# Scaling x in place ahead of plain transposes, with later weight splits and two store queues, in a two-layer decoder trunk

## The chip, the cores and the metric

The kernel runs on one core of a Trainium2 chip. The metric is the device time of one execution in microseconds (us). TensorE multiplies matrices and transposes, VectorE and ScalarE do elementwise work, GpSimd fills constants, and SyncE (SP) issues the DMAs. Each engine takes its instructions in the order in which the code issues them.

## What is computed

A trunk of two residual layers on x of 256 tokens by 2048 channels, batch 1. Layer 0 is an RWKV-7 token mixer, layer 1 a differential attention; each has a gate path and an output projection. Only the start of layer 0 and the very end matter here:

```python
def rms_norm(x, w, eps):
    y = xf * lax.rsqrt(jnp.mean(xf * xf, axis=-1, keepdims=True) + eps)
    return y * w
...
h = rms_norm(x, norm_w[i], NORM_EPS)
h_prev = jnp.pad(h, ((0, 0), (1, 0), (0, 0)))[:, :T]
xs = h[None] + (h_prev - h)[None] * mu[:, None, None, :]      # six mixed inputs
proj = jnp.einsum('pbtd,dpe->pbte', jnp.stack([x_r, x_k, x_v, x_g]), w_in.reshape(D, 4, RWKV_WIDTH))
...
x = x + y                                                     # after each layer
return rms_norm(x, final_norm_w, NORM_EPS)
```

## The kernel before

**The large products.** A weight tile holds 2 x 128 rows by 512 columns of a weight matrix. `fetch` loads it from DRAM on SP's queue, `high` (ScalarE, L196) casts it to a short type, `low` (VectorE) makes the remainder, and a product step multiplies high and low parts: 24 matmuls of 128 x 256 in layer 0's first products. `gemm` runs eight such steps for one block of 512 output columns. `RAW` = 4 raw tiles and `LEAD` + 1 = 4 split tiles are held. In step `i0`, `gemm` first fetches tile `i0 + 5`, then issues the matmuls, then `high(i0 + LEAD)`, then a piece of each live stream (`pump`), then `low(i0 + LEAD)`.

**The operand of the first products.** x lies in `xin` with tokens on the partitions, in two blocks of 128 tokens, t = 0 and 1. ScalarE squares it as its loads land, and the root of the mean gives `rs0`, one factor for each token. For each pair kp of 128-channel blocks (eight pairs), a generator `first_pairs` does three pieces of work, here called flip, mix and finish:

- `flip(kp)`: TensorE brings the pair to channels on the partitions, into a PSUM bank; ScalarE copies it to `ht` (L310). Before the change the flip is a plain matmul of x with the diagonal matrix `rsd`, which holds `rs0`, so that it scales and transposes at once. The two diagonals are made by VectorE directly after `rs0`.
- `mix`: for two blocks, ScalarE multiplies by one factor (L314) and VectorE adds the block shifted by one token times another.
- finish: ScalarE casts the pair to the short type (L326) and VectorE makes the remainder; only then is the pair an operand of a product step.

**The order around it.** `staggered` starts one pair with each call. So one call issues the finish of pair n - 2, the mix of pair n - 1 and the flip of pair n, in that order, on all engines. VectorE's instructions go through a wrapper and all bear line L95; matmuls bear L103, transposes L107. The manual schedule keeps the order of the code on each engine. Four small VectorE instructions that prepare the layer's parameters (`par`, `omu`) stand after `rs0` and the diagonals and before the first call. The calls before the first product are:

```python
    next(first)                       # call 1: flip 0
    low(0)
    next(first)                       # call 2: mix 0, flip 1
    next(first)                       # call 3: finish 0, mix 1, flip 2
    for i in range(1, LEAD):
        high(i)
        low(i)
        if i + 1 < LEAD:
            fetch(RAW - 1 + i)
        next(first)                   # calls 4 and 5
```

The later calls come one in each product step, as the stream of rank 0. When `first_pairs` is through, the stream `lora` begins, and other streams (keys, inverses, queries, the scan) follow it beside the products. The planner `clock` adds up a price of each instruction for TensorE and VectorE, and a stream's piece waits while VectorE is too far behind by it.

**The end.** `finish(t, ps)` adds the last product, takes the final norm of 128 tokens and scales four blocks of 512 columns, two on ScalarE (L1095) and two on VectorE, and SP stores them (L1099).

Of the kernel before, what the change touches and what calls it, by code (L numbers as in the profile page):

```python
# [11 lines left out]
AF = mybir.ActivationFunctionType  # L12
ALU = mybir.AluOpType
AX = mybir.AxisListType

P = 128
D = 2048
T = 256
# [14 lines left out]
BANKS = {"gm": 2, "ka": 2, "qa": 2, "xy": 1, "us": 1}  # L33
LEAD = 3        # weight tiles split ahead of the products
RAW = 4         # weight tiles held as they come from DRAM
NR = 6          # queries whose matrices are held for the scan
LIMITS = (9, 9, 3, 4, 2.5, 3)   # by rank of a stream: VectorE's allowed arrears in us at the end of its next piece


@with_exitstack  # L40
def rwkv_diff_trunk(ctx, tc, x, norm_w, mu, w_in, w0, w1, w2, a0, a1, a2, k_k, k_a, r_k, ln_w, ln_b,
# [39 lines left out]

    # What TensorE and VectorE have been given so far, in us at about the price of each instruction by its shape:
    # the order of issue is chosen by it.
    clock = {"pe": 0.0, "dve": 0.0}
# [23 lines left out]

    # ---------------------------------------------------------------- streams of work beside the large products
    # A stream yields after each piece; every step of a large product is followed by one piece of each live  # L110
    # stream, so that what a piece waits for was issued a whole step earlier. It yields about what its next piece
    # costs VectorE in us; the piece waits while VectorE is too far behind for the stream's rank. A negative price:
    # the next piece waits for nothing of another engine and may follow in the same step.
    live, done, stores = [], set(), []
# [39 lines left out]

    # ---------------------------------------------------------------- inputs and constants
    xin = L([P, NT, D], "xin")
    xr = x[0].rearrange("(t p) d -> p t d", p=P)
    halves = [slice(q * 1024, (q + 1) * 1024) for q in range(2)]
    prm = L([P, P], "prm")
    for q in halves:  # L160
        for t in range(NT):
            DMA.dma_start(xin[:, t, q], xr[:, t, q])
    DMA.dma_start(prm[0:32, :], norm_w.rearrange("l (k p) -> (l k) p", p=P))
    DMA.dma_start(prm[32:128, :], mu[0].rearrange("s (k p) -> (s k) p", p=P))

    # ---------------------------------------------------------------- weights, in the order of use
    plan = []
# [25 lines left out]
    def high(i):  # L193
        if i < len(plan):
            his[i] = S([P, 2, 512], "whi", LEAD + 1, F32R)
            A.copy(his[i], raws[i])  # L196

    def low(i):
        if i < len(plan):
            los[i] = S([P, 2, 512], "wlo", LEAD + 1, F32R)  # L200
            V.tensor_tensor(los[i], raws[i], his[i].bitcast(F32), op=ALU.subtract)
# [27 lines left out]
    def gemm(xs, n, tok, evac, each=None):  # L229
        ps = [big_bank(), big_bank()]  # L230
        for kp in range(n):
# [6 lines left out]
            for o in range(2):  # L238
# [3 lines left out]
                for i in range(2):  # L242
                    first, last = kp == 0 and i == 0, kp == n - 1 and i == 1
                    for b in range(2):
# [4 lines left out]
                        mm(o_, lo[:, i, sl], xk[:, 0, i, :], start=False, stop=last and b == 1)  # L249
            high(i0 + LEAD)  # L250
            if kp == n - 1:
# [3 lines left out]
            pump()  # L255
            low(i0 + LEAD)

    # ---------------------------------------------------------------- constants
    zb = S([P, P], "zb", 1, mybir.dt.bfloat16)
# [9 lines left out]

    # ---------------------------------------------------------------- layer 0: norm  # L270
    def rms_scale(ss, n, tag):
# [4 lines left out]

    ss0 = S([P, 2, NT], "ss0")
    ht = S([P, KT, T + 1], "big")
    V.memset(ht[:, :, 0:1], 0.0)
    for i, q in enumerate(halves):  # L280
        for t in range(NT):
            sq = L([P, 1024], "sq", 2)
            A.activation(sq, xin[:, t, q], AF.Square, accum_out=ss0[:, i, t:t + 1])
    V.tensor_tensor(ss0[:, 0, :], ss0[:, 0, :], ss0[:, 1, :], op=ALU.add)
    rs0 = rms_scale(ss0[:, 0, :], D, "rs0")
    rsd = L([P, NT, P], "rsd")
    for t in range(NT):
        V.tensor_scalar(rsd[:, t], ident, rs0[:, t:t + 1], None, op0=ALU.mult)
    high(0)
# [14 lines left out]
    def flip(kp):  # L304
        ps = I(("ka", "qa")[kp % 2])
        for i in range(2):
            for t in range(NT):
                mm(ps[:, i * T + t * P:i * T + (t + 1) * P], xin[:, t, (2 * kp + i) * P:(2 * kp + i + 1) * P],
                   rsd[:, t], start=True, stop=True)
        A.copy(ht[:, 2 * kp:2 * kp + 2, 1:T + 1], ps.rearrange("p (i t) -> p i t", i=2))  # L310
# [21 lines left out]

    # ---------------------------------------------------------------- spills between the products and the streams
    def spill(shape, tag):
# [26 lines left out]

    # ---------------------------------------------------------------- LoRA down projections
    tw = S([LORA + 1, T], "tw")
# [32 lines left out]

    # ---------------------------------------------------------------- keys: decay, scaled k and b, chunk matrices
    gs, wss, zfs = [dict() for _ in range(NG)], {}, {}
# [85 lines left out]

    # ---------------------------------------------------------------- inverses of the unit triangular chunk matrices
    def inverse(j):
# [61 lines left out]

    # ---------------------------------------------------------------- queries: [a, r] per chunk, masked score matrices

# [55 lines left out]

    # ---------------------------------------------------------------- scan over the chunks
    def scans():
# [73 lines left out]

    # ---------------------------------------------------------------- gate path, group norm, bonus
    ys = {}
# [96 lines left out]

    # ---------------------------------------------------------------- layer 0 products
    xs = {p: [] for p in (0, 2, 3, 5)}
# [11 lines left out]
    low(0)  # L795
    next(first)
    next(first)
    for i in range(1, LEAD):
        high(i)
        low(i)  # L800
        if i + 1 < LEAD:
            fetch(RAW - 1 + i)
        next(first)

# [101 lines left out]

    # ---------------------------------------------------------------- layer 1: differential attention
    def row_scale(ss, tag):
# [179 lines left out]
    def finish(t, ps):  # L1088
        V.tensor_tensor(acc[3][:, t], ps, acc[3][:, t], op=ALU.add)
        squares(3, t)  # L1090
        tot = L([P, 1], "rs2t", 2)
        V.tensor_reduce(tot, ss2[:, t], axis=AX.X, op=ALU.add)
        rs2 = rms_scale(tot, D, f"rs2{t}")
        for cb in (0, 1):
            A.activation(acc[cb][:, t], acc[cb][:, t], AF.Copy, scale=rs2)  # L1095
        V.tensor_scalar(acc[2][:, t], acc[2][:, t], rs2, None, op0=ALU.mult)
        V.scalar_tensor_tensor(acc[3][:, t], acc[3][:, t], rs2, fws[3], op0=ALU.mult, op1=ALU.mult)
        for cb in (2, 0, 3, 1):
            DMA.dma_start(out[0, t * P:(t + 1) * P, 512 * cb:512 * cb + 512], acc[cb][:, t])  # L1099

# [49 lines left out]
```

## Time and profile before

| what | us |
|---|---|
| median of 3 runs | 1166.25 |
| lowest and highest run | 1165.7 and 1166.59 |
| span of the profiled execution, first to last instruction | 1161.7 |
| median less that span (start and end of an execution, outside the span) | 4.55 |
| TensorE busy in the span | 1139.3 |
| VectorE busy | 801.1 |
| ScalarE busy | 616.8 |

The profile is of one execution. A matmul's row starts when it starts; matmuls overlap, so the time from one start to the next is what one costs in a series. The same holds for VectorE and ScalarE, whose next instruction starts a little before the last one's end. The granted clock of TensorE stands as a share of 2.4 GHz: 1.00 or 0.50 (1.2 GHz). One fp32 matmul has two rows, one plain transpose has one.

### The profile page before, as it was taken

To read this page: it belongs to the slowest core of one execution; us is meant where nothing else is said; L and a number is where in the kernel's file an instruction comes from. 1 tells how busy PE (TensorE), PEld (TensorE's weight loads), DVE (VectorE), ACT (ScalarE), POOL (GpSimd) and SP (SyncE) were. 2 spreads that over 40 slices of the span, in tenths; PEclk is the share of its full clock that TensorE was granted. 3 is DMA by queue.
4 is the path that set the end of the run, shared out by engine and by line. 5 is a ranking of instruction groups with operands and counts; after the bars stand their busy time and mean duration, and the time that the engine had idled before them with its cause. 6 is when DMAs were issued, how large, how long until landed. Compare 5 with 4: busy or idle time off the path is not lost.

```text
span 1161.7 us, 21253 instructions
## 1 busy us (share of the span) xinstructions
PE 1139.3 (98%) x8426; PEld 994.8 (86%) x8426; DVE 801.1 (69%) x1316; ACT 616.8 (53%) x1032; POOL 13.9 (1%) x38
## 2 busy tenths in 40 slices
PE   8999999999999999999999999999999999999996
PEld 6999998998788787888878899899889889987885
DVE  5755889989788768777796664466456647646764
ACT  7655854556533555355544543455446445545643
POOL 1020000000000000000000000000000000000000
PEclk9999999999999899999999999999999999999999
DMA  8646768876656538666585566654755665564463
GB/s 260 196 150 206 216 183 255 240 221 196 187 164 200 156 123 268 184 172 189 163 272 182 180 195 193 192 152 146 206 159 162 185 178 146 176 201 150 150 231 108
DMA packets 140820, 217.63 MB, mean 187 GB/s; under 512 B 29793, under 2 KB 45490, under 8 KB 140722
## 3 DMA queue, kind: packets, MB, share of 16 engines
q1 hardware_dynamic: 140722, 216.28, 61.2%
q8 instruction: 66, 1.08, 0.4%
q14 instruction: 32, 0.26, 0.1%
HBM read 197.37 MB, written 18.87 MB: 186 GB/s over the span
## 4 chain that ended last, share of the span: by engine, by line
PE 89%; DVE 5%; DMA 3%; issue 1%; ACT 1%; SPq 0%; ACTq 0%; DVEq 0%
PE gm L103 59%; PE us L103 16%; PE ka L103 5%; PE qa L103 4%; PE xy L103 4%; DVE wlo L95 2%; PE qa L107 1%; DMA xin<-in_x_dram 1%; PE ka L107 1%; DVE wp L95 1%; DVE ev L95 0%; PE xy L107 0%; DVE zf L95 0%; DMA ws<-yd 0%; DMA rd<-ev 0%
## 5 line engine op out<-in xcount | busy, mean ns | idle before, releaser
L95 DVE TENSOR_TENSOR wlo<-wraw,whi 128x1024 fp32r<-128x1024 f32 x320 | 389.1, 1221 | 116.9 <-ACT whi L196 116.2
L196 ACT CAST whi<-wraw 128x1024 fp32r<-128x1024 f32 x320 | 333.4, 1044 | 200.1 <-PE gm L103 134.8
L103 PE MATMUL gm<-whi,xs 128*128 128x512 f32 x944 | 321.5, 405 | 1.5 <-DVE acc L95 0.7
L103 PE MATMUL gm<-xs,whi 128*128 128x256 f32 x1376 | 256.2, 286 | 0.0
L103 PEld LDWEIGHTS gm<-xs,whi 128*128 128x128 f32 x1376 | 214.1, 189 | 3.4 <-issue 1.3
L103 PEld LDWEIGHTS gm<-whi,xs 128*128 128x128 f32 x944 | 178.0, 189 | 44.4 <-issue 1.5
L103 PE MATMUL gm<-xs,wlo 128*128 128x256 f32 x688 | 194.9, 283 | 0.5 <-DVE wlo L95 0.5
L103 PE MATMUL gm<-wlo,xs 128*128 128x512 f32 x472 | 185.2, 392 | 0.0
L103 PEld LDWEIGHTS gm<-xs,wlo 128*128 128x128 f32 x688 | 129.6, 188 | 0.9 <-DVE wlo L95 0.9
L103 PEld LDWEIGHTS gm<-wlo,xs 128*128 128x128 f32 x472 | 89.3, 189 | 18.5
L103 PE MATMUL gm<-xt,whi 128*128 128x256 f32 x352 | 64.2, 283 | 0.0
L103 PE MATMUL gm<-whi,xt 128*128 128x512 f32 x176 | 58.1, 390 | 0.0
L103 PEld LDWEIGHTS gm<-xt,whi 128*128 128x128 f32 x352 | 53.7, 188 | 1.3 <-issue 1.3
L103 PE MATMUL gm<-xt,wlo 128*128 128x256 f32 x176 | 49.3, 280 | 0.0
L103 PEld LDWEIGHTS gm<-whi,xt 128*128 128x128 f32 x176 | 33.0, 188 | 7.6
L975 ACT ACTIVATE sc<-sc,mxx 128x128 f32<-128x128 f32 (+1 forms) x64 | 28.4, 446 | 18.1 <-DVE mxx L95 18.1
L103 PEld LDWEIGHTS xy<-uv,G 128*64 128x64 f32 (+1 forms) x512 | 32.2, 136 | 5.8 <-issue 1.8
L103 PE MATMUL xy<-uv,G 128*64 128x64 f32 (+1 forms) x512 | 36.6, 223 | 0.0
L103 PE MATMUL gm<-wlo,xt 128*128 128x512 f32 x88 | 34.7, 394 | 0.0
L677 ACT COPY uv<-xy 64x512 f32<-64x512 f32 x16 | 9.3, 581 | 46.6 <-PE xy L103 46.6
L103 PEld LDWEIGHTS gm<-xt,wlo 128*128 128x128 f32 x176 | 33.1, 188 | 0.0
L314 ACT ACTIVATE ev<-big,omu 128x256 f32<-128x256 f32 x64 | 29.1, 502 | 3.7 <-DMA rd<-ev 2.1
(265 smaller groups left out, 1675.8 us busy)
## 6 DMA issues: line engine op xcount, KB each, us to landing
wraw<-in_rwkv_w_in_dram SPq DMA_DIRECT2D x128, 512.0 KB
wraw<-in_diff_w_in_dram SPq DMA_DIRECT2D x128, 512.0 KB
wraw<-in_rwkv_w_out_dram SPq DMA_DIRECT2D x32, 512.0 KB
wraw<-in_diff_w_out_dram SPq DMA_DIRECT2D x32, 512.0 KB
bkd<-bkc SPq DMA_DIRECT2D x16, 256.0 KB
bkq<-bkd SPq DMA_DIRECT2D x16, 256.0 KB
xin<-in_x_dram SPq DMA_DIRECT2D x4, 512.0 KB
kd<-ev SPq DMA_DIRECT2D x8, 256.0 KB
```

What stands on the lines that cost most here:

```text
L95: return fn(*args, **kw)
L103: PE.matmul(out, lhsT, rhs, start=start, stop=stop)
L107: PE.transpose(out=out, in_=in_, identity=identity)
L196: A.copy(his[i], raws[i])
L314: A.activation(m, ht[:, k, 1:T + 1], AF.Copy, scale=omu[:, col:col + 1])
L677: A.copy(ye, xy[64:128, :])
L975: A.activation(sc[:, m, b0:b1], sc[:, m, b0:b1], AF.Exp, bias=mx[:, t, m:m + 1], accum_out=sm[:, t, m:m + 1])
```

## The change

It has four parts. The loads of x become five: the second half of block t = 1 comes as two pieces, with a square for each, so `ss0` has three columns for each block and a reduce adds them. The diagonal `rsd` goes: `flip` has VectorE scale the columns of x in place by `rs0` and TensorE transpose them plainly; pairs 0 and 1 are scaled one at a time (256 columns of each token block), later ones two at a time (512 columns, with the even pair). Only three calls, not five, and two split weight tiles, not three, stand ahead of the first product; step 0 then splits tile 2, step 1 tiles 3 and 4, and later steps one tile each as before. At the end ScalarE issues the stores of the two blocks that it scales, each directly after its scaling; SP keeps the other two.

```diff
-    for q in halves:
-        for t in range(NT):
-            DMA.dma_start(xin[:, t, q], xr[:, t, q])
+    parts = [(t, slice(a, b)) for a, b, ts in ((0, 1024, (0, 1)), (1024, 2048, (0,)), (1024, 1536, (1,)),
+                                               (1536, 2048, (1,))) for t in ts]
+    for t, q in parts:
+        DMA.dma_start(xin[:, t, q], xr[:, t, q])
...
-            high(i0 + LEAD)
+            split = range(2, 3) if i0 == 0 else range(3, 5) if i0 == 1 else (i0 + LEAD,)
+            for i in split:
+                high(i)
...
-            low(i0 + LEAD)
+            for i in split:
+                low(i)
...
-    ss0 = S([P, 2, NT], "ss0")
+    ss0 = S([P, NT, 3], "ss0")
+    nc.gpsimd.memset(ss0, 0.0)
...
-    V.tensor_tensor(ss0[:, 0, :], ss0[:, 0, :], ss0[:, 1, :], op=ALU.add)
-    rs0 = rms_scale(ss0[:, 0, :], D, "rs0")
-    rsd = L([P, NT, P], "rsd")
-    for t in range(NT):
-        V.tensor_scalar(rsd[:, t], ident, rs0[:, t:t + 1], None, op0=ALU.mult)
+    sst = S([P, NT], "sst")
+    V.tensor_reduce(sst, ss0, axis=AX.X, op=ALU.add)
+    rs0 = rms_scale(sst, D, "rs0")
...
     def flip(kp):
         ps = I(("ka", "qa")[kp % 2])
+        w = 1 if kp < 2 else 2
+        if kp < 2 or kp % 2 == 0:
+            for t in range(NT):
+                cols = xin[:, t, 2 * kp * P:2 * (kp + w) * P]
+                V.tensor_scalar(cols, cols, rs0[:, t:t + 1], None, op0=ALU.mult)
         for i in range(2):
             for t in range(NT):
-                mm(ps[:, i * T + t * P:i * T + (t + 1) * P], xin[:, t, (2 * kp + i) * P:(2 * kp + i + 1) * P],
-                   rsd[:, t], start=True, stop=True)
+                transpose(out=ps[:, i * T + t * P:i * T + (t + 1) * P],
+                          in_=xin[:, t, (2 * kp + i) * P:(2 * kp + i + 1) * P], identity=ident)
...
     next(first)
     low(0)
     next(first)
+    high(1)
     next(first)
-    for i in range(1, LEAD):
-        high(i)
-        low(i)
-        if i + 1 < LEAD:
-            fetch(RAW - 1 + i)
-        next(first)
+    low(1)
+    fetch(RAW)
...
+        def put(queue, cb):
+            queue.dma_start(out[0, t * P:(t + 1) * P, 512 * cb:512 * cb + 512], acc[cb][:, t])
+
         for cb in (0, 1):
             A.activation(acc[cb][:, t], acc[cb][:, t], AF.Copy, scale=rs2)
+            put(A, cb)
         V.tensor_scalar(acc[2][:, t], acc[2][:, t], rs2, None, op0=ALU.mult)
         V.scalar_tensor_tensor(acc[3][:, t], acc[3][:, t], rs2, fws[3], op0=ALU.mult, op1=ALU.mult)
-        for cb in (2, 0, 3, 1):
-            DMA.dma_start(out[0, t * P:(t + 1) * P, 512 * cb:512 * cb + 512], acc[cb][:, t])
+        for cb in (2, 3):
+            put(DMA, cb)
```

## Rows read from the trace of the kernel before

**Rows 1.** The page: span, and busy time of each engine.
```profile
span 1161.7 us, 21253 instructions
...
PE 1139.3 (98%) x8426; PEld 994.8 (86%) x8426; DVE 801.1 (69%) x1316; ACT 616.8 (53%) x1032; POOL 13.9 (1%) x38
```

**Rows 2.** Chain of waits, first 60 us: start us, us, what.
```profile
9.90 1.16 ACT sq L283 x2
...
12.29 1.16 PE ka L103 x8
...
17.76 0.89 PE ka L103 x8
18.65 2.83 PE gm L103 x24
...
29.81 14.22 PE gm L103 x120
```

**Rows 3.** Timeline of ScalarE: start us, us, instruction, idle time before it.
```profile
8.46 1.06 ACT L283 ACTIVATE sq<-xin 128x1024 f32<-128x1024 f32 x1 [0.90 <-DMA xin<-in_x_dram]
...
13.48 0.59 ACT L310 COPY big<-ka 128x512 f32<-128x512 f32 x1 [0.91 <-PE ka L103]
...
15.56 0.62 ACT L326 CAST xs<-ev 128x512 fp32r<-128x512 f32 x1
...
16.89 0.56 ACT L310 COPY big<-ka 128x512 f32<-128x512 f32 x1
17.36 1.04 ACT L196 CAST whi<-wraw 128x1024 fp32r<-128x1024 f32 x1
```

**Rows 4.** Timeline of VectorE, the same columns.
```profile
11.67 0.17 DVE L95 RECIPROCAL rs<-rs 128x2 f32<-128x2 f32 x1 [0.42 <-ACT rs L273]
11.95 0.48 DVE L95 TENSOR_SCALAR rsd<-ident,rs 128x128 f32<-128x128 f32 x2
12.34 0.28 DVE L95 COPY par<-xy 128x128 f32<-128x128 f32 x1
...
13.25 1.22 DVE L95 TENSOR_TENSOR wlo<-wraw,whi 128x1024 fp32r<-128x1024 f32 x1
14.65 0.88 DVE L95 SCALAR_TENSOR_TENSOR ev<-big,par,ev 128x256 f32<-128x256 f32 x2 [0.18 <-ACT ev L314]
```

**Rows 5.** Windows: us, busy by engine, the granted clock (PEclk), DMA share, GB/s.
```profile
core 0: us, PE busy (x) PEld busy (x) DVE busy (x) ACT busy (x) POOL busy (x), PEclk, DMA share, GB/s
8.40:12.20 3.80, 0.30 (x1) 0.14 (x1) 0.58 (x4) 3.16 (x6) 0.00 (x0) 1.00 1.05 386
13.00:13.50 0.50, 0.50 (x7) 0.50 (x6) 0.50 (x3) 0.01 (x1) 0.00 (x0) 0.99 1.05 385
13.50:16.50 3.00, 3.00 (x16) 3.00 (x15) 2.14 (x4) 2.94 (x7) 0.00 (x0) 0.50 1.12 286
16.50:17.00 0.50, 0.50 (x4) 0.50 (x4) 0.50 (x2) 0.50 (x3) 0.00 (x0) 0.59 1.18 317
397.40:399.90 2.50, 0.00 (x0) 0.00 (x0) 2.14 (x5) 1.14 (x3) 0.00 (x0) 0.86 0.77 215
400.00:405.90 5.90, 5.90 (x74) 4.96 (x75) 1.57 (x2) 3.53 (x6) 0.00 (x0) 0.50 0.36 105
406.00:406.50 0.50, 0.50 (x4) 0.31 (x2) 0.00 (x0) 0.00 (x0) 0.00 (x0) 0.97 0.00 0
```

**Rows 6.** Timeline of the end, VectorE, ScalarE and SP's queue.
```profile
1155.44 1.34 ACT L1095 ACTIVATE acc<-acc,rs 128x512 f32<-128x512 f32 x2 [0.23 <-DVE rs L95]
1155.44 0.49 DVE L95 TENSOR_SCALAR acc<-acc,rs 128x512 f32<-128x512 f32 x1
1155.84 0.75 DVE L95 SCALAR_TENSOR_TENSOR acc<-acc,rs,y 128x512 f32<-128x512 f32 x1
1155.95 1.80 SPq L1099 DMA_DIRECT2D out_dram<-acc  x4
```

**Rows 7.** Timeline of TensorE in layer 0's output products: four transposes, then a product.
```profile
634.10 0.60 PE L107 MATMUL ka<-ident,acc 128*128 128x128 f32 x4
634.46 0.48 PE L103 MATMUL gm<-whi,xs 128*128 128x512 f32 x1
```

More of the change, by code (lines that the diff above doesn't have):

```diff
@@ L157, in rwkv_diff_trunk @@
     xr = x[0].rearrange("(t p) d -> p t d", p=P)
-    halves = [slice(q * 1024, (q + 1) * 1024) for q in range(2)]
+    parts = [(t, slice(a, b)) for a, b, ts in ((0, 1024, (0, 1)), (1024, 2048, (0,)), (1024, 1536, (1,)),
+                                               (1536, 2048, (1,))) for t in ts]
     prm = L([P, P], "prm")
-    for q in halves:
-        for t in range(NT):
-            DMA.dma_start(xin[:, t, q], xr[:, t, q])
+    for t, q in parts:
+        DMA.dma_start(xin[:, t, q], xr[:, t, q])
     DMA.dma_start(prm[0:32, :], norm_w.rearrange("l (k p) -> (l k) p", p=P))
@@ L275, in rms_scale @@
         return r
-    ss0 = S([P, 2, NT], "ss0")
+    ss0 = S([P, NT, 3], "ss0")
+    nc.gpsimd.memset(ss0, 0.0)
     ht = S([P, KT, T + 1], "big")
     V.memset(ht[:, :, 0:1], 0.0)
-    for i, q in enumerate(halves):
-        for t in range(NT):
-            sq = L([P, 1024], "sq", 2)
-            A.activation(sq, xin[:, t, q], AF.Square, accum_out=ss0[:, i, t:t + 1])
-    V.tensor_tensor(ss0[:, 0, :], ss0[:, 0, :], ss0[:, 1, :], op=ALU.add)
-    rs0 = rms_scale(ss0[:, 0, :], D, "rs0")
-    rsd = L([P, NT, P], "rsd")
-    for t in range(NT):
-        V.tensor_scalar(rsd[:, t], ident, rs0[:, t:t + 1], None, op0=ALU.mult)
+    col = [0, 0]
+    for t, q in parts:
+        sq = L([P, 1024], "sq", 2)
+        A.activation(sq[:, 0:q.stop - q.start], xin[:, t, q], AF.Square, accum_out=ss0[:, t, col[t]:col[t] + 1])
+        col[t] += 1
+    sst = S([P, NT], "sst")
+    V.tensor_reduce(sst, ss0, axis=AX.X, op=ALU.add)
+    rs0 = rms_scale(sst, D, "rs0")
     high(0)
```

## The prediction

> **What bounds the kernel now.** I read the page first. TensorE is busy 1139.3 of 1161.7 us [rows 1], so a change can matter only where TensorE stands idle, where its clock is low, or where its own work shrinks. All parts of this one lie in the first 50 us and the last 8 us, so I read the chain of waits of the start next [rows 2]. The reader is to see three stretches: x arrives and is squared until 11.06 us (the last square takes 1.16 from 9.90 with its read-out); the five flips that are issued ahead of the first product run from 12.29 to 18.65; from there TensorE never stops, eight steps of 2.83 us with the last three flips between them, and the eighth step ends at 29.81 + 14.22 = 44.03. The third view is the two engines that feed it, as queues [rows 3, 4]. Their rows stand in the order of the code (copy 0, mix 0, copy 1, cast 0, ... on ScalarE), so an instruction late in its queue holds all behind it. The fourth is the granted clock [rows 5]: 1.00 (2.4 GHz) to nearly 13.5 us, 0.50 (1.2 GHz) until 16.5, and back during the next half us.
>
> **Parts that cost about nothing.** Splitting the last x load makes five loads of the same bytes. The third square starts at 8.46 [rows 3] and with the same 1.16 ends at 9.62; two half squares, which I estimate at 0.73 each (half of the 1.06 and a read-out of some 0.2), then end at 11.08 instead of 11.06. I take 0; bounds are -0.5 (all of the last piece earlier by one half square) and +0.45 (one more issue on SP at the price of [rows 6]). The three-column sum replaces an add of the same size: 0. Later weight loads wait for later splits, but those tiles are wanted later too, by more than their splits slip in the walk below: 0, and covered by the products in between.
>
> The last stores: at the end ScalarE scales two blocks in 1.34 us from 1155.44, and SP issues four stores in 1.80 us from 1155.95, 0.45 each, until 1157.75 [rows 6]. SP now has two and would finish about 0.7 earlier. But on ScalarE the store of block 0 stands in the queue ahead of the scaling of block 1. So ScalarE's series is 0.67 (scale) + 0.45 (issue) + 0.67 + 0.45 = 2.24, plus 0.1 of waits, from 1155.44: 1157.8. I price an issue on ScalarE by SP's row, since no DMA is issued there before. The tail gains 0; bounds -0.7 and +0.5. The Trainium skill (DMA: Bandwidth & Descriptors, "Issuing engines are not separate DMA queues") says that a second issuing engine saves only the issue time. By that rule alone the tail would give two issues back, about 0.9 us, and the sum below would be 9.95.
>
> **The flips themselves.** One flip was eight matmul passes, 0.89 us at full clock [rows 2]. A plain transpose is one pass: four take 0.36 us, from 634.10 to the next matmul at 634.46, with some 0.08 lost behind them [rows 7]; I take 0.40. So a flip costs TensorE 0.4 to 0.5 us less.
>
> **Where the order turns.** The old diagonal cost VectorE two instructions, 0.48 us at 11.95, ahead of everything else [rows 4], and every flip could follow at once. Now each flip waits for its columns to be scaled, in VectorE's queue. 512 columns cost 0.49 us, and the next instruction starts 0.40 later (1155.84, the partner of the row at 1155.44) [rows 6]; two of 128 columns took 0.48 together, 0.19 to the next [rows 4]. For 256 columns, between the two, I take 0.30 and 0.21, near the lower end. All ten are 4 x 0.21 + 6 x 0.40 = 3.2 us of VectorE, 2.8 net; if TensorE's own work hid this, it would cost nothing. It is not hidden, because of what is queued ahead. Walked through, with the durations of these queues [rows 3, 4] and about 0.04 per handover:
>
> First scaling: the four parameter instructions, which ran from 12.34 until the split at 13.25, behind the diagonal [rows 4], now stand ahead. They start after the reciprocal at 11.77 and free VectorE at 12.68; the two scalings end at 13.19. Flip 0 runs from 13.23 at half clock, and copy 0 starts at 14.09 (13.48 before). Second scaling: it stands behind mix 0. From copy 0 to the end of mix 0 on VectorE took 13.48 to 15.53, 2.05 us [rows 3, 4], so now to 16.14; two scalings, 16.56; flip 1, at half clock, 17.6. Copy 1 starts at 17.63; before, TensorE had flip 1 ready early and copy 1 ran straight behind mix 0. Behind copy 1 on ScalarE stand the second weight cast (1.04 long, 0.95 to the next) and cast 0, which makes the operand of the first product: cast 0 starts at 17.63 + 0.47 (a copy's slot, 16.89 to 17.36) + 0.95 = 19.05 instead of 15.56 [rows 3]. Then mix 1 from 19.58, its second VectorE half until 21.18, two 512-column scalings until 21.99, flip 2 at half clock 0.8 us. The first product starts at 22.82 against 18.65: **+4.17**, though only three flips stand ahead of it instead of five.
>
> Clock: TensorE works some 2.4 of the 9.6 us before that. In the trace the clock fell just before 13.5, after a stretch of 3.8 us with 0.30 of work, and rose at 16.9 (0.59 is the mean of that half us), 4.6 us after steady work began at 12.29 [rows 2]. In the stop from 397.4 to 399.9 it fell near 399.2 (the mean is 0.86), and it rose at 406.0, 6.0 us after work began at 400.0 [rows 5]. So I let the first product begin at half clock and the clock rise at about 28.0, half of 5.2 us: **+2.6** (bounds 0 and +3.0). The Trainium skill (TensorE: Matmul & The Clock Gate, "Part 4: PE-mode transpose") states that transposes do not count as busy for this gate. By it the transposes could not bring the clock back before 22.8, which is the +2.6 above; if they did count, the time would be that of the first rival. No transpose of the trace stands in a stretch of low clock, so no row here decides it.
>
> Steps: the lead of five flips is three, and cast k+2 now stands on ScalarE behind copy k+3, which waits for flip k+3, which stands behind product k. Product 1 ends at 31.5. Ahead of product 2 stands flip 4, which needs a scaling: copy 3 at 28.9, then two weight casts (this is where the split takes two tiles in one step), cast 2 at 31.25, mix 3 from 31.8, its VectorE end at 33.3, two scalings until 34.2. TensorE waits **+2.75**. The same for flip 6 ahead of product 4, with one weight cast: **+1.8**. The odd flips find their columns scaled; two small waits behind flip 7 make **+0.2**. Before the change three flips of 0.89 stood between the products, now five of 0.40: **-0.67**.
>
> Sum: 4.17 + 2.6 + 2.75 + 1.8 + 0.2 - 0.67 = 10.85, so the eighth step ends near 54.9. The same walk on the old order gives 18.65 for the first product and 43.96 for the end, against 44.03 in the trace. TensorE is nearly full from there to the end, so the delay passes through. The profiled span of 1161.7 becomes 1172.55; the median of the runs, 1166.25, stands 4.55 above that span, and I add the same: **1177.1 us**.
>
> What I cannot price: the LoRA stream starts two steps later and every later piece is placed by the planner, so the stops further in, such as the one at 397.4 [rows 5], may move, shrink or grow. That stop cost some 2.6 idle and 3.0 at half clock; I allow one such stop gained or added, 5.6 each way.
>
> **Rivals.** (1) *Clock back early*: it is up before the first product. For it: it rose amid flips before. Against: those were unbroken work. 10.85 - 2.6 - 0.7 (flips at full clock, and with them the copies) = +7.5: 1173.8. (2) *Clock falls a second time* in the wait before product 2: that wait of 2.75 is as long as the stop at 397.4, which was followed by 6.0 us of half clock. Another half of 4.6 to 6.0, so 2.6: 1179.7. Against: in that stop the clock fell only 1.8 us in, so the length is marginal. (3) *Faster: the scalings run ahead of the mixes*, so that only TensorE's path counts. The first product then waits for its operand alone: copy 0 at about 13.6, cast 0 and its subtraction end near 17.2, so -1.45 at 18.65; three flips at 0.89 then become five at 0.40, -0.67 again, and no waits follow, plus 0.5 because the clock then rises later. That gives -1.6: 1164.6. It decides if flip 1's scaling starts before mix 0 ends on VectorE. Against it speaks that every row of VectorE stands in code order [rows 4]. (4) *Hidden anyway*: the later stops give back about 11 us, 1166.3; these stops together are hardly that large.
>
> **How the numbers follow.** The sum as it stands has 0.54, (1) 0.15, (2) 0.17, (3) 0.05, (4) 0.04; 0.05 is left for a new stop worse than these. The time given is that of the first. Its own range is 1174.5 to 1177.5 by the clock's bounds. The range given runs from (1) less 4.3 to (2) plus 3.8, each about three quarters of a moved stop: 1169.5 to 1183.5; (3), (4) and the worse stop lie outside. The tail's other price by the issue time, 0.9 less, has 0.1 in each case and carries none over a bound. A difference under 0.2%, some 2.3 us, is about what this measurement cannot tell from none. (3) and (4) lie within 0.2% by their sums, and half of each may fall beyond it: slower 0.91, same 0.05, faster 0.04.
>
> **What would show it.** Right: the first product at 22 to 23 us; copy 1 some 2 us after mix 0 and cast 0 near 19 on ScalarE; TensorE waiting for the scaling before flips 4 and 6 but not 5 and 7; clock 0.50 into the first product; the eighth step ending at 53 to 57; the last issue still near 2.3 us after the last reciprocal. Wrong: a first product before 18.65, scalings that run ahead of mix 0, or a delay that is in place at 55 us and is gone by 600.

## The result, and the profile after

The kernel with the change takes 1178.64 us (median of 4 runs, 1177.54 to 1180.96) against 1166.42 for the kernel before (4 runs, 1165.70 to 1166.85). The ratio is 1.0111 [1.0098, 1.0123], with its 95% interval in brackets: slower by 12.2 us by the medians and 12.9 by the ratio, where 10.85 was forecast. The profiled execution took 1177.54 us with a span of 1175.8, so 1.74 us lie outside its span. In the kernel before it is about 2.2 us: 2.15 to 2.27 in every execution of it that was run beside the experiments. The execution profiled before [rows 1] was therefore one of about 1163.9, some 2.5 us short of the median of its kernel. So of the 4.55 us that stand in the table as "outside the span", only some 2.2 lie there. The two spans differ by 14.1.

The page after: span, and busy time of each engine. TensorE's work is the same [rows 1]; what is new is time in which it stands idle or runs at half clock.

```profile
span 1175.8 us, 21200 instructions
...
PE 1140.3 (97%) x8394; PEld 994.1 (85%) x8394; DVE 804.7 (68%) x1324; ACT 617.2 (52%) x1034; POOL 14.8 (1%) x39
```

The chain of waits after, from mix 0 to flip 7, answers to [rows 2]:

```profile
15.11 0.88 DVE ev L95 x2
16.00 0.27 DVE xin L95
16.32 1.18 PE qa L107 x4
17.52 0.58 ACT big L318
18.11 0.94 ACT whi L196
19.05 0.53 ACT xs L334
19.60 0.69 DVE xs L95
20.29 0.79 DVE ev L95 x2
21.08 0.41 DVE xin L95
21.54 1.30 PE ka L107 x4
22.84 4.42 PE gm L103 x24
27.26 0.45 PE qa L107 x4
...
33.10 0.90 PE ka L107 x3
34.00 4.01 PE gm L103 x24
38.00 0.45 PE qa L107 x4
...
42.90 0.55 PE ka L107 x3
43.44 2.85 PE gm L103 x24
46.30 0.44 PE qa L107 x4
```

Read it link by link. The second scaling (`xin`, 16.00) stands behind mix 0 (`ev`), flip 1 (`qa`) behind that scaling, copy 1 (`big`) behind flip 1, and the weight cast (`whi`) and cast 0 (`xs`, ScalarE) behind copy 1. Then the same again: cast 0's remainder, mix 1, the third scaling, flip 2, and only then the first product at 22.84. Before, the chain held five flips in a row there. The last six rows are flip 4 to flip 5 and flip 6 to flip 7, with the products 2 and 4 in between; flips 5 and 7 follow their product at once.

The timeline of TensorE after shows the same waits from its side: the flips that stood idle for their columns, with the idle time ahead of each in brackets. The row at 32.75 names no engine ("issue"), but VectorE's two scalings for this flip ran from 32.16, 0.88 us together.

```profile
12.75 1.17 PE L107 MATMUL ka<-ident,xin 128*128 128x128 f32 x4 [2.28 <-DVE xin L95]
16.32 1.17 PE L107 MATMUL qa<-ident,xin 128*128 128x128 f32 x4 [2.40 <-DVE xin L95]
21.54 1.30 PE L107 MATMUL ka<-ident,xin 128*128 128x128 f32 x4 [4.05 <-DVE xin L95]
32.75 1.25 PE L107 MATMUL ka<-ident,xin 128*128 128x128 f32 x4 [2.21 <-issue]
42.59 0.85 PE L107 MATMUL ka<-ident,xin 128*128 128x128 f32 x4 [1.32 <-DVE xin L95]
```

The windows of the start after (columns as in [rows 5]) show the clock: 0.50 from flip 0 into the first product, up after 26.2, down again at 33.1 behind the wait of 2.21, and up after 36.4.

```profile
8.00:12.30 4.30, 0.30 (x1) 0.14 (x1) 1.02 (x6) 3.60 (x8) 0.00 (x0) 1.00 1.06 399
12.70:22.70 10.00, 3.50 (x13) 2.32 (x14) 5.90 (x12) 4.35 (x8) 0.00 (x0) 0.50 0.88 270
22.80:26.20 3.40, 3.40 (x18) 3.40 (x17) 1.46 (x4) 2.86 (x5) 0.00 (x0) 0.50 0.50 148
26.30:33.00 6.70, 4.49 (x37) 4.16 (x36) 3.51 (x8) 3.80 (x6) 0.00 (x0) 1.00 0.27 79
33.10:36.40 3.30, 3.30 (x16) 3.30 (x17) 2.50 (x3) 2.37 (x5) 0.00 (x0) 0.50 0.32 47
```

Where the first block's sum is read out marks the end of the eighth step. This is the read-out of its second half on ScalarE, before and then after, 11.48 us later:

```profile
44.12 0.58 ACT L349 COPY ev<-gm 128x512 f32<-128x512 f32 x1 [0.89 <-PE gm L103]
```
```profile
55.60 0.59 ACT L357 COPY ev<-gm 128x512 f32<-128x512 f32 x1 [0.91 <-PE gm L103]
```

The end after answers to [rows 6]:

```profile
1169.06 0.16 DVE L95 RECIPROCAL rs<-rs 128x1 f32<-128x1 f32 x1 [0.36 <-ACT rs L276]
1169.26 0.72 ACT L1103 ACTIVATE acc<-acc,rs 128x512 f32<-128x512 f32 x1 [0.23 <-DVE rs L95]
...
1169.77 0.99 SPq L1100 DMA_DIRECT2D out_dram<-acc  x2
1170.01 0.34 ACTq L1100 DMA_DIRECT2D out_dram<-acc  x1
1170.39 0.72 ACT L1103 ACTIVATE acc<-acc,rs 128x512 f32<-128x512 f32 x1 [0.41 <-ACT acc L1103]
1171.14 0.34 ACTq L1100 DMA_DIRECT2D out_dram<-acc  x1
```

SP is done at 1170.76, but ScalarE's second scaling starts only behind its first store. From the last reciprocal to the end of the last issue it is 2.42 us (1171.48 less 1169.06), and was 2.51 (1157.75 [rows 6], less the start of the reciprocal before):

```profile
1155.24 0.17 DVE L95 RECIPROCAL rs<-rs 128x1 f32<-128x1 f32 x1 [0.36 <-ACT rs L273]
```

### The profile page after: what moved, and what is told of

Same layout as the page of the kernel before. It is cut to its first block, busy times and chain, and to the rows that moved or that the text cites. A ratio compares the mean times of both kernels' runs of the same rounds, so it can differ in the third digit from the quotient of the medians.

```text
span 1175.8 us, 21200 instructions
## 1 busy us (share of the span) xinstructions
PE 1140.3 (97%) x8394; PEld 994.1 (85%) x8394; DVE 804.7 (68%) x1324; ACT 617.2 (52%) x1034; POOL 14.8 (1%) x39
## 3 DMA queue, kind: packets, MB, share of 16 engines
q8 instruction: 66, 1.08, 0.4%
## 4 chain that ended last, share of the span: by engine, by line
PE 92%; DVE 2%; ACT 2%; DMA 2%; issue 1%; SPq 0%; ACTq 0%; DVEq 0%
PE gm L103 62%; PE us L103 15%; PE ka L103 4%; PE xy L103 4%; PE qa L103 4%; PE qa L107 1%; PE ka L107 1%; DMA wraw<-in_rwkv_w_out_dram 1%; DMA xin<-in_x_dram 1%; ACT whi L196 1%; DVE wlo L95 0%; PE xy L107 0%; DMA rd<-ev 0%; DVE wp L95 0%; DVE ev L95 0%
## 5 line engine op out<-in xcount | busy, mean ns | idle before, releaser
L103 PE MATMUL gm<-xs,whi 128*128 128x256 f32 x1376 | 261.1, 289 | 0.0
L103 PEld LDWEIGHTS gm<-xs,whi 128*128 128x128 f32 x1376 | 217.7, 192 | 3.7 <-issue 1.3
L95 DVE TENSOR_TENSOR xs<-ev,xs 128x512 fp32r<-128x512 f32 x32 | 22.1, 690 | 23.4 <-ACT xs L334 23.3
```

The lines of the kernel that those rows point to most:

```text
L95: return fn(*args, **kw)
L103: PE.matmul(out, lhsT, rhs, start=start, stop=stop)
```

## The experiments

The theory: what costs is the place of the scalings in VectorE's queue, behind the mixes; the low clock follows from those waits. The rivals: the shorter lead of three calls, the loads and stores, the clock alone, or the streams that start two steps later. All ratios are to the kernel before, run on the same chip. No kernel leaves out any part of the computation.

**1. The old lead (is it the shorter lead?).** The change with five calls and three split tiles ahead of the first product, as before:

```diff
-            split = range(2, 3) if i0 == 0 else range(3, 5) if i0 == 1 else (i0 + LEAD,)
+            split = (i0 + LEAD,)
...
+    for i in range(1, LEAD):
+        high(i)
+        low(i)
+        if i + 1 < LEAD:
+            fetch(RAW - 1 + i)
+        next(first)
```

> The changed kernel with the old lead: five calls and three split weight tiles ahead of the first product, one tile per step. Theory (the scaling queued behind the mixes on VectorE is what costs): the flips ahead of the first product stay in series, so the first product starts later still, at 29 to 31 us instead of 22.8, but then with its operands far ahead and without the two waits; the eighth step ends at 54 to 56, as in the changed kernel (55.5), and the time is within 1.5 us of it. Rival (the short lead is what costs, plain transposes are innocent): first product near 18, eighth step at 44 to 45, time near 1167.

Measured: 1179.39 us, 1.0114 [1.0095, 1.0134], the same as the change. The wait is only elsewhere: TensorE stands 6.60 us before flip 4, which is now ahead of the first product, and still 1.30 before flip 6, which had not been expected. The read-out is at 57.83 instead of 55.60, later than the expected 54 to 56, and yet the time is no longer (the streams start in their old step here; run 7 has what that is worth). With plain flips the lead isn't the cause, nor a remedy. What it costs with diagonal ones is in run 6.

**2. The old flip with the new lead (is it the plain flip?).** `rsd` is back, the scalings are gone:

```diff
-        w = 1 if kp < 2 else 2
-        if kp < 2 or kp % 2 == 0:
-            for t in range(NT):
-                cols = xin[:, t, 2 * kp * P:2 * (kp + w) * P]
-                V.tensor_scalar(cols, cols, rs0[:, t:t + 1], None, op0=ALU.mult)
...
-                transpose(out=ps[...], in_=xin[...], identity=ident)
+                mm(ps[...], xin[...], rsd[:, t], start=True, stop=True)
```

> The changed kernel with the old flip through the diagonal, and all else of the change: three calls ahead, later splits, five loads, two store queues. Theory: flips wait for no scaling, first product at 17.5 to 18, one small wait or none, eighth step at 45 to 46.5; time 1 to 2.5 us above the kernel before. Rival (the short lead and the two splits in one step cost): waits before the products 2 and 4 as in the changed kernel, eighth step beyond 50, time 6 us or more above the kernel before.

Measured: 1169.42 us, 1.0033 [1.0021, 1.0045]. So the plain flip with its scalings accounts for 7.8 of the 11.1 thousandths, 9.1 us. The read-out is at 46.32, 2.2 after that of before. The loss of 3.8 us by the ratio is more than the expected 1 to 2.5; what goes beyond the 2.2 arises later (run 7).

**3 and 4. The scalings taken out of the mixes' way.** Run 3 has all ten scalings ahead of the first transposes. Run 4 has only those of flips 0 to 3 there, and leaves flips 4 and 6 as the change has them, so that the terms of the sum come apart:

```diff
-        if kp < 2 or kp % 2 == 0:
-            for t in range(NT):
-                cols = xin[:, t, 2 * kp * P:2 * (kp + w) * P]
+        if kp == 0:
+            for k0, k1 in ((0, 2), (2, 4), (4, 8), (8, 12), (12, 16)):
+                for t in range(NT):
+                    cols = xin[:, t, k0 * P:k1 * P]
```

and in run 4 the two lines that choose the columns are one:

```diff
+        for k0, k1 in {0: ((0, 2), (2, 4), (4, 8)), 4: ((8, 12),), 6: ((12, 16),)}.get(kp, ()):
```

> The changed kernel with all ten scalings issued together ahead of the first transposes instead of one pair at a time. Same work on every engine. Theory: flips 1 and 2 run straight behind flip 0, the first product starts near 19.2, no wait before flips 4 and 6, eighth step at 45 to 46; time 9 to 10.5 us below the changed kernel, 0 to 2.5 above the kernel before. Rival (plain transposes or scaled columns are slow in themselves, or the clock alone costs): gain under 4 us.

> The changed kernel with the six scalings of flips 0 to 3 ahead of the first transposes; the scalings of flips 4 and 6 stay where the change has them. Theory (the terms of the sum add up one by one): the first product starts near 18 us, as with all ten ahead, so the +4.17 is gone; TensorE still waits about 2.2 us before flip 4 and 1.3 before flip 6, and the first block's products end about 3 us later than with all ten ahead, near 49.5 against 46.4; time 1174 to 1175.5. Rival (only the first product's start counts, the later waits are taken up by other slack): near 46.5, and the time within 1 us of that with all ten ahead, 1171.6.

Measured: 1171.61 us for all ten, 1.0046 [1.0031, 1.0061], less gain than expected; 1173.61 for six, 1.0062 [1.0040, 1.0084], 0.4 under what was expected. The timeline of TensorE in run 4 shows the first product at 17.12, and both waits before flips 4 and 6 in place, as long as in the change:

```profile
17.12 1.30 PE L103 MATMUL gm<-xs,whi 128*128 128x256 f32 x2 [1.82 <-ACT xs L333]
...
28.98 0.90 PE L107 MATMUL ka<-ident,xin 128*128 128x128 f32 x4 [2.17 <-issue]
...
38.82 0.85 PE L107 MATMUL ka<-ident,xin 128*128 128x128 f32 x4 [1.32 <-DVE xin L95]
```

In run 3 both are gone. The read-outs are at 55.60 (the change), 51.78 (six ahead) and 47.87 (all ahead): 3.8 us for the scalings of the first flips, 3.9 for the later two. In run 4 the first product starts 5.7 us earlier than in the change, but it runs at half clock from beginning to end (17.12 to 22.91; the granted clock is 0.50 in the windows from 17 to 23), so that only 3.8 are left at the read-out. All ten ahead are no remedy, for two reasons. They hold VectorE from 12.26 for 3.51 us, so mix 0 comes to VectorE at 16.83 (15.11 in the change). And the clock stays low through the whole first product, as the windows of run 3 show:

```profile
12.70:18.30 5.60, 2.84 (x12) 2.36 (x12) 5.00 (x12) 3.48 (x7) 0.00 (x0) 0.50 1.13 328
18.50:24.30 5.80, 5.65 (x25) 5.36 (x26) 5.13 (x8) 3.41 (x7) 0.00 (x0) 0.50 0.73 221
24.50:28.00 3.50, 3.50 (x33) 3.49 (x31) 0.02 (x1) 3.05 (x5) 0.00 (x0) 1.00 0.51 154
```

Run 2, with diagonal flips and the same lead, has its clock back before its first product at 17.80:

```profile
12.70:17.40 4.70, 4.67 (x22) 4.37 (x21) 2.24 (x5) 3.20 (x6) 0.00 (x0) 0.50 1.11 323
17.60:24.00 6.40, 5.86 (x47) 5.67 (x48) 5.24 (x8) 5.27 (x11) 0.00 (x0) 1.00 0.85 251
```

**5. The change with its waits filled (is it the clock?).** TensorE multiplies constant zeros while it waits; nothing reads that product. The first loop stands ahead of the first flip, the second ahead of flips 4 and 6, the third behind flips 0 and 1:

```diff
+    for _ in range(20):
+        PE.matmul(warm, zb, zb[:, 0:1].broadcast_to([P, 512]), start=True, stop=True)
...
+        for _ in range({4: 9, 6: 5}.get(kp, 0)):
+            PE.matmul(warm, zb, zb[:, 0:1].broadcast_to([P, 512]), start=True, stop=True)
...
+        for _ in range((13, 18, 0, 0)[min(kp, 3)]):
+            PE.matmul(warm, zb, zb[:, 0:1].broadcast_to([P, 512]), start=True, stop=True)
```

> The changed kernel with matmuls on constant zeros put into TensorE's waits (20 more ahead of flip 0, 13 behind flip 0, 18 behind flip 1, 9 ahead of flip 4, 5 ahead of flip 6), so that the clock has no cause to fall; all else alike, the planner's sums too. Theory (half clock is a large part of the loss, through the flips as well as the first product): clock 1.00 from 13 to 55 us, first product at 21.4 instead of 22.5, eighth step at 50 to 51 instead of 55.5, time 4 to 5.5 us below the changed kernel. Rival (only the first product's own half-speed time counts, 2.6): 2 to 3 us below. Second rival (the clock costs nothing, the queues set the pace): within 1 us.

Measured: 1174.59 us, 1.0085 [1.0071, 1.0098]. The ratio gives 3.0 us less than the change, the medians 4.05: between the two expectations. The windows show a clock of 1.00 in all that the change ran at half:

```profile
12.70:22.70 10.00, 9.03 (x46) 4.82 (x48) 6.56 (x15) 4.53 (x9) 0.00 (x0) 1.00 0.87 264
22.80:26.20 3.40, 3.40 (x32) 3.40 (x31) 1.81 (x5) 2.97 (x6) 0.00 (x0) 1.00 0.52 152
```

The first product still starts at 22.24 (21.4 was expected), and the read-out is at 52.06, 3.5 earlier. Part of the gain is lost to the zero products themselves. They stand ahead of the transpose of the layer's parameters in TensorE's queue, which ran at 10.17 in the change, and flip 0, at 12.75 there, comes 0.66 later:

```profile
11.79 0.27 PE L107 MATMUL xy<-ident,prm 128*128 128x128 f32 x1
13.41 0.81 PE L107 MATMUL ka<-ident,xin 128*128 128x128 f32 x4 [1.35 <-DMA wraw<-in_rwkv_w_in_dram]
```

So the low clock is at least 3 to 4 us of the loss, and the waits themselves are the greater part of the rest.

**6. The loads and the two store queues alone**, on the kernel before:

```diff
+    parts = [(t, slice(a, b)) for a, b, ts in ((0, 1024, (0, 1)), (1024, 2048, (0,)), (1024, 1536, (1,)),
+                                               (1536, 2048, (1,))) for t in ts]
...
+            put(A, cb)
```

> The kernel before with only the small parts of the change: five loads of x with a square each, and half of the last stores from ScalarE. Theory: squares end about 0.3 us earlier, the end is unchanged, first product at 18.3; time within 1 us of the kernel before. Rival (stores from ScalarE save their issue time): 0.9 us more, time 1.2 below the kernel before; or the second queue adds a wait of 0.5 at the end.

Measured: 1164.49 us, 0.9988 [0.9976, 1.0000]. The reciprocal of the first norm is at 11.36, 0.31 earlier [rows 4]. At the end, last reciprocal to last issue is 2.43 us (1156.92 to 1159.35): no gain, as in the change. The read-out is at 43.76, 0.36 earlier than before.

This kernel differs from run 2 only by the lead and the order of the splits, so the two show what the short lead costs with diagonal flips: 1.0033 less 0.9988, 5.2 us, with 2.56 of it there at the read-out (46.32 less 43.76); the rest holds the later streams of run 7. With plain flips, in run 1 and the change, the same step makes no difference in the time, since the first product there waits for the scalings with either lead.

**7. The LoRA stream started in its old step**, with the diagonal flip (run 2) and in the change itself:

```diff
-        yield from staggered([first_pairs(kp) for kp in range(KT // 2)], lambda n: True, 1)
-        start(lora(), 1)
+        for n, price in enumerate(staggered([first_pairs(kp) for kp in range(KT // 2)], lambda n: True, 1)):
+            if n == 8:
+                start(lora(), 1)
+            yield price
```

> The changed kernel with the old diagonal flips, as in the run at 1169.42 us, but the LoRA stream starts in the product step in which it started before the change. Theory (part of that run's loss of 3 to 3.5 us over the kernel before is the shift of all streams by two steps): the stop near 182 us is back at about 2.0 from 2.8, the second stretch of low clock behind it goes, and the time is 1 to 2 us below that run, 1167.4 to 1168.4. Rival (the loss is all at the start): within 0.7 us of 1169.4.

> The changed kernel, except that the LoRA stream starts in the product step in which it started before the change. If the shift of the streams by two steps costs what lies between the delay at 54 us (11.5) and the delay at the end (14.1), the stops of 3.15 near 192 and 1.17 near 292 us shrink and the time falls by 1 to 2.5 us, to about 1176.5 to 1177.5. Rival (these stops come from the late start alone, or move elsewhere): within 0.7 us of 1178.6.

Measured: 1167.68 us, 1.0013 [1.0001, 1.0026], and 1176.74 us, 1.0098 [1.0084, 1.0111]; 1.7 and 1.9 us below their partners by the medians. The stop inside the scan's work shows why, by what ends it. First the change, then the change with the old start of LoRA:

```profile
195.13 1.16 PE L103 MATMUL qa<-cont,bkq 64*128 64x128 f32 x16 [3.15 <-DMA cont<-ard]
```
```profile
196.62 1.16 PE L103 MATMUL qa<-cont,bkq 64*128 64x128 f32 x16 [2.39 <-DVE pr L95]
```

With the streams two steps late, TensorE waits there for a DMA; otherwise for VectorE, 0.76 less, as the kernel before did (1.97). The same in run 2: 2.82 for the DMA, then 1.93 for VectorE. But the low clock behind the stop didn't go, as had been expected for the first of these runs: it is 0.50 from 188.25 to 195.0. The two profiled spans show no gain of that size (0.1 us longer and 0.3 shorter than those of their partners), and the intervals overlap a little.

The other runs bear out what ends the stop. In all six kernels whose streams start two steps late (the change and runs 2, 3, 4, 5 and 8) it is a DMA, after 2.82 to 3.92 us; in the other eight it is VectorE, after 1.91 to 2.99. An estimate from all ratios, each less what its read-out explains: behind the read-out the six late kernels lose 1.3 us to the kernel before in the mean, and the seven others gain 0.4 on it. So the shift likely costs 1.5 to 2 us; as a time it isn't settled.

**8. The scalings on GpSimd**, off VectorE's queue:

```diff
-                V.tensor_scalar(cols, cols, rs0[:, t:t + 1], None, op0=ALU.mult)
+                nc.gpsimd.tensor_scalar(cols, cols, rs0[:, t:t + 1], None, op0=ALU.mult)
```

> The changed kernel with the ten scalings on GpSimd instead of VectorE, nothing else moved. GpSimd has nothing queued then. Theory (the place in VectorE's queue costs, not the scaling): flip 1 follows flip 0 without waiting for mix 0 unless GpSimd itself takes over 1 us for 256 columns, first product at 17.5 to 19, no wait of TensorE before flips 4 and 6, eighth step at 44 to 47, time 7 to 10 us below the changed kernel. Rival (scaling x in place and plain transposes cost as such): gain under 4 us.

Measured: 1170.73 us, 1.0048 [1.0034, 1.0062], 7.3 us (6.3 thousandths) less than the change. GpSimd is slow at it. Its timeline has the six scalings of flips 0 to 3, and TensorE's has flip 0 cut in two by the second of them:

```profile
11.64 7.59 POOL L313 TENSOR_SCALAR xin<-xin,rs 128x256 f32<-128x256 f32 x6 [9.59 <-DMA wraw<-in_rwkv_w_in_dram]
```
```profile
12.66 0.47 PE L107 MATMUL ka<-ident,xin 128*128 128x128 f32 x1 [2.24 <-POOL xin L313]
14.41 0.90 PE L107 MATMUL ka<-ident,xin 128*128 128x128 f32 x3 [1.27 <-POOL xin L313]
```

The first product starts at 19.84 and the read-out is at 48.36, both later than the theory had them (17.5 to 19, 44 to 47), and flip 4 still waits 0.53 for its second scaling. Even so it beats VectorE's quick scalings, since GpSimd's stand behind no mix: the read-out is 7.2 earlier than in the change.

**9. The same with the old lead, all stores from SP, and the wait ahead of the first flip filled:**

```diff
+    for _ in range(20):
+        PE.matmul(warm, zb, zb[:, 0:1].broadcast_to([P, 512]), start=True, stop=True)
...
+            split = (i0 + LEAD,)
...
+        for cb in (2, 0, 3, 1):
+            DMA.dma_start(out[0, t * P:(t + 1) * P, 512 * cb:512 * cb + 512], acc[cb][:, t])
```

> Plain transposes with the scalings on GpSimd, the old lead of five flips and the old splits, stores on SP's queue, and the 20 bridging matmuls. Theory: the flips cost 0.45 instead of 0.89 us and wait only for GpSimd; if it keeps up (under 1.4 us for 512 columns of one block), first product at 16.5 to 18 and eighth step at 40.5 to 42, time 2 to 4 us below the kernel before. Rival (GpSimd is too slow): the first product waits for flip 4 behind ten scalings, beyond 20, time above the kernel before.

Measured: 1170.52 us, 1.0044 [1.0031, 1.0056], not the 2 to 4 us below the kernel before of the theory but the rival's case: eight scalings before the first product take GpSimd 11.40 us, and the product starts at 23.66.

**10. A version that beats both: the kernel before with five loads and the gap ahead of its first flips filled** by twenty more of the zero products that stand there already:

```diff
+    for _ in range(20):
+        PE.matmul(warm, zb, zb[:, 0:1].broadcast_to([P, 512]), start=True, stop=True)
```

> The kernel before with the five loads of x, its own stores on SP's queue, and 20 more matmuls on constant zeros ahead of the first flip, which bridge the stop in which x is still awaited. Theory: no half clock in the five flips, first product at 16.6 to 17 instead of 18.4, eighth step near 42, time 1.5 to 2.5 us below the kernel before. Rival (the half clock at the start is hidden by the wait for the operand): first product still near 18, time within 0.7 us of the version with five loads alone.

Measured: 1162.84 us, 0.9978 [0.9968, 0.9987]. Its clock stays at 1.00 until 183.7, where that of before was at half from 13.5 to 16.9; the first product starts at 16.77 and the read-out is at 42.53, 1.59 before that of the kernel before. Against run 6, which has the five loads without the filling, the read-out is 1.23 earlier; the intervals of the two times overlap, so how much of the gain is the filling is not settled as a time.

**11. Plain flips where the scaling is not in the way.** Run 10, with flips 5 to 7 plain and their scalings behind mixes 0 to 2, several steps ahead of use. (The expectation counts these mixes from 1. It also names two store queues, but in runs 10 and 11 all four stores stay on SP.)

```diff
+                if kp < 5:
+                    mm(ps[...], src, rsd[:, t], start=True, stop=True)
+                else:
+                    transpose(out=ps[...], in_=src, identity=ident)
+        if 1 <= kp <= 3:
+            for t in range(NT):
+                cols = xin[:, t, 2 * (kp + 4) * P:2 * (kp + 5) * P]
+                V.tensor_scalar(cols, cols, rs0[:, t:t + 1], None, op0=ALU.mult)
```

> The kernel before with five loads, two store queues and the bridging products of the run that stood at 1162.84 us, but flips 5 to 7, which stand between the product steps, are plain transposes; their 256-column scalings stand on VectorE behind mixes 1, 2 and 3, five steps ahead of their use. Theory (it is the place of the scaling in VectorE's queue that costs, not the plain transpose): nothing waits for these scalings, the first product stays at 16.8 us, three flips of 0.45 replace three of 0.89, and the time falls by 1.0 to 1.3 us, to about 1161.7. Rival (VectorE has no room there either): the remainders behind the scalings slip, the first product comes 0.5 or more later, and the time is that of the run without them or more, 1162.8 to 1164.

Measured: 1164.12 us, 0.9985 [0.9976, 0.9994]: no gain over run 10 (their intervals overlap), the rival's time, but not by its mechanism. TensorE's timeline in this run shows a flip that costs 0.35 us to the next product; in run 10 it costs 0.81 (19.81 to 20.62):

```profile
19.46 0.60 PE L107 MATMUL qa<-ident,xin 128*128 128x128 f32 x4
19.81 0.54 PE L103 MATMUL gm<-xs,whi 128*128 128x256 f32 x2
```

No flip waits, and the read-out is at 41.45, 1.08 earlier. Of this, 0.36 is there at the start of the first product and has another cause: in run 10 flip 0 follows the forty zero products and the parameters' transpose at 12.38 without a wait, while here these are through earlier (the first twenty took 5.97 us instead of 7.02) and flip 0 starts at 11.92, as soon as its diagonal is ready. The gain is lost further in: the stop near 180 us is 2.99 instead of 2.32, and one of 0.76 near 315 is new. Why the later pieces fall so stays open.

## Why the prediction was right, and where its sizes were off

The time lay 1.5 us above the forecast, inside the range, and the mechanism was the one given, with part of rival (2) added. Part of the closeness is luck. The forecast was a span of 1172.55 and 4.55 us on top. The profiled span came out at 1175.8, 3.25 above; but the 4.55 held some 2.3 us by which the execution profiled before was short, and after the change the median stands only 2.84 above the profiled span, which gives 1.71 of the 3.25 back. The terms, measured from the rows after and the read-outs:

| term | forecast | measured | how |
|---|---|---|---|
| first product's start | +4.17 | +4.19 | 22.84 less 18.65 |
| clock, first product | +2.6 | +1.59 | 4.42 less 2.83 |
| clock, flip 4 and product 2 | 0 | +1.63 | 4.01 less 2.83, and 0.90 less 0.45 |
| wait before flip 4 | +2.75 | +2.56 | 30.54 to 34.00, less the flip's 0.90 |
| wait before flip 6 | +1.8 | +1.69 | 41.30 to 43.44, less 0.45 |
| cheaper flips | -0.67 | -0.42 | 5 x 0.45 less 3 x 0.89 |
| small waits | +0.2 | +0.24 | what is left; no wait is listed behind flip 7 |
| eighth step | +10.85 | +11.48 | 55.60 less 44.12 |

The two ends of products that the table needs, 30.54 and 41.30, are the starts of products 1 and 3 (27.71 and 38.45) plus 2.83 and 2.85.

**The place in the queue was right.** Copy 1 was forecast 17.63 and came at 17.52; cast 0 at 19.05 and came at 18.95; flips 4 and 6 wait, 5 and 7 don't. The run with six scalings ahead shows the two halves of the sum separately, and the run with the old lead shows that with plain flips nothing hangs on the lead. That the first product's start fits to 0.02 us is luck in part, because errors cancel. A flip at half clock took 1.17 to 1.30 us and not the 0.8 to 1.0 of the walk; but a flip starts behind the first of its two scalings (flip 2 at 21.54, where both end at 21.88), and the loads started everything 0.3 earlier.

**The clock's step was mis-sized in both directions.** I let the clock rise at about 28.0; it rose at 26.2, so the first product lost 1.59 and not 2.6. And it fell a second time, at about 33.1, right behind the wait of 2.21 before flip 4. That was rival (2), at 0.17, with a price of 2.6 more; it measured 1.63, since the clock came back after 3.4 us. The two together make 3.2 where the sum had 2.6, so the errors of -1.0 and +1.6 partly cancel; filling the waits gave 3 to 4 back. The likeliest case's own range, up to 1177.5, did not hold the time, because it left the second fall to a rival. The Trainium skill (TensorE: Matmul & The Clock Gate, "Part 4: PE-mode transpose") says that a transpose does not count as busy in the same way as a matmul. The runs agree: through plain flips the clock stayed at half into the first product (here, and in runs 3, 4 and 8), through diagonal ones it was back before it. Since TensorE also stood idle between or behind the plain flips, that is no proof.

**Loads at nothing, tail at nothing.** The loads gave 0.3 us at the first reciprocal, inside the bounds of -0.5 and +0.45. The 0.4 us that went from outside the span (2.2 before, 1.7 to 1.9 in every version with five loads, run 6 too) have no term in the sum, and no run shows their cause. The tail's last issue moved by 0.09, so the store on ScalarE's queue did hold back the second scaling, as walked; an issue there took 0.34, not the 0.45 taken from SP. By the rule of the Trainium skill (DMA: Bandwidth & Descriptors, "Issuing engines are not separate DMA queues"), that a second issuing engine saves the issue time, the sum would be 0.9 lower. That gain did not appear, neither here nor in run 6.

**Downstream.** "The delay passes through" held as a first answer, as no later stop gave it back. But the spans differ by 14.1, 2.6 more than at the read-out. One part is the streams' shift, which I had left unpriced: the stop near 192 us waits for a DMA instead of VectorE (run 7). By the medians, and with the 0.4 that went from outside the span, the spans differ by about 12.6 only, so part of the 14.1 belongs to the two executions that were profiled. Where that part lies isn't shown; both kernels have a stop and a stretch of low clock near 400 us [rows 5].

**Rival (3) was priced wrongly.** All scalings ahead of the mixes were to give 1164.6; run 3 has that order and took 1171.61. Its first product started at 18.41, where the rival had 17.2: mix 0 had to wait for 3.5 us of scalings. And the clock was at half for all of the first product.

## What to carry to other kernels

Work that is taken off the busiest engine and put on another one is paid for at its place in that engine's queue, not by its duration: scalings of 3.5 us in all made the end of the eighth step 9.3 us later (55.60 against 46.32 with the diagonal in the same order), because they stood behind mixes that themselves waited for the flips before. Before folding a scale out of a matmul, list what stands ahead of the new instruction on its engine and what that waits for; if the list leads back to the consumer, the pipeline has become a chain. And where TensorE is nearly full, price a new wait of some 2 us twice, as idle time and as the half clock that may follow it (it did after the 2.21 us before flip 4; it did not after the 1.32 before flip 6, nor after the stop of 1.97 near 183 us in the kernel before). And look at the gaps that are there already: the versions that beat both kernels clear of noise, runs 10 and 11, have one of them filled, and the five loads.

## What the runs showed of the hardware that was not expected

- The same scaling costs GpSimd several times what it costs VectorE: six took 7.59 us on GpSimd (four of 256 columns, two of 512), all ten took 3.51 on VectorE (four of 256, six of 512).
- A DMA issue took 0.34 us on ScalarE's queue; on SP's two took 0.99.
- A wait of 2.21 us, at the end of a stretch at full clock (26.3 to 33.0), was followed by 3.3 us at half clock (33.10 to 36.40), though TensorE was busy throughout those 3.3.
